# Ten product pairs instead of eight, lookup tables in shared slots, and new planner numbers in a one-core attention block

## The chip, the cores and the metric

The kernel runs as one program on one core of one Trainium2 chip. The time is device microseconds of one execution; lower is better. One core has a tensor engine (PE) with its weight loads (PEld), a vector engine (DVE), a scalar engine (ACT), GpSimd (POOL) and a sync engine (SP) that here issues nearly all DMAs. The engines run their own instruction lists in order and wait for each other through semaphores.

## What is computed

One pre-norm residual block on x (512 tokens x 1024 channels, float32). One projection of the normalised input gives the parts of two attention branches and of their gates; branch A is dense latent attention, branch B keeps the 128 best keys of each query by an indexer's score. The reference, cut to what matters:

```python
h = rmsnorm(x, norm_g[l])
(q_lat, c_kv, k_rope, z_a, q_b, k_b, v_b, z_b,
 q_idx, k_idx, w_idx, gate_a, gate_b) = jnp.split(h @ w_in[l], cuts, axis=-1)
...
y_a = mla_attention(q_nope, q_pe, k_nope, k_pe, v_a, pos) * silu(z_a)
y_b = dsa_attention(q_b, k_b, v_b, q_idx, k_idx, w_idx, rel_bias, pos, topk) * silu(z_b)
merged = sigmoid(gate_a) * (y_a @ w_o_a[l]) + sigmoid(gate_b) * (y_b @ w_o_b[l])
x = x + merged @ w_out[l]
return rmsnorm(x, final_g)
```

## The kernel before

**Precision.** Every float32 operand of a product is split into a rounded high part and the rest (`split_w` L728, `lo_part` L471): ACT writes the high part, DVE or POOL subtracts to get the low part. A product is then three matmuls, high x high, high x low, low x high (`mm3` L500). Activations have channels on the partitions and 512 tokens along the row.

**Single and paired tiles.** A projection tile of 128 output columns taken alone (`proj` L1154) is 8 blocks of channels x 3 = 24 matmuls of 512 columns. Two tiles taken together (`proj2` L1218, `seven` L1304) go through a scheme of seven half-size products instead of eight: 7 x 4 x 3 = 84 matmuls of 256 columns for both. For that, DVE and POOL form sums of weight blocks (`prep` L1243: four additions of 512 columns a pair) and split seven weight blocks where two single tiles have four; the sums of the input are made once (`input_sums` L1185, tiles `s_hs`). ACT and DVE collect the four results in tiles called `s_pair`. The values of branch B (`values2` L1356, VB) are a pair of the same kind with four outputs.

**Stages in the order of time.** Loads of x and of the early weights; indexer scores (`scores` L955) and the choice of keys (`topk` L979: 16 rounds of MAX8 and MATCH_REPLACE for each of three query tiles, on DVE); eight dense heads (`mla_head`, matmuls L1909 to L1911, their row maximum on DVE in L1893); eight sparse heads (`dsa_head`, its row minimum on DVE in L1992); the branch output products (`branch_out`, tiles `s_ys`); the last projection (`output`, tiles `s_wo` and `s_mg`), norm and store. Between the attention matmuls, PE takes projection tiles as filler. The sparse heads start once all three masks are chosen.

**What sets the order.** A planner (`Flow` L154) runs while the program is built. Each piece of work is a Python generator that yields steps; a step has a modelled duration on each engine that may take it. The planner repeatedly emits the step that can start first, with a small tie-break by priority (`PHEAD`, `PSCORE`, `PFILL`, `PTOPK`). So the order of every engine's list follows from the modelled durations, the priorities and the buffers: a shared pool of `NSLOT` = 73 slots of 128x512 floats with caps by use (`WCAP`, `PCAP`, `PHCAP`, `TCAP`, `SPARE`), four raw buffers of 128x1024 for weight loads (`fetcher` L1118), and eight PSUM banks. The modelled PE time is in `stream` (L485), `mm` and `turn` (L507). The order of the projection tiles is the string `QUEUE`: lower case is a single tile, capitals are pairs (SB is the pair of a key and a query tile of branch B).

**Operands of a dense head.** A head's query and key tiles get their rotary rows by small DMAs: `qhi` and `s_op` tiles from `s_th`, `s_op`, `s_qpe` and the shared `kpeh`, `kpel` (`mla_job`). All stand in SP's list, between the weight loads (`raw<-w_...`) and the spills of finished gates to HBM (`bias_scratch<-s_sig`).

Of the kernel before, what the change touches and what calls it, by code (L numbers as in the profile page):

```python
# [36 lines left out]
MARK = -3.4e38  # L37
BIG = 2.0 ** 127
LOW = -(2.0 ** 126)
NSLOT = 73  # L40
NRAW = 4


# [257 lines left out]
def tile_block(ctx: ExitStack, tc: tile.TileContext, a: dict, out: bass.AP, bias_dram: bass.AP):  # L301
# [13 lines left out]
    def fixed(name, shape, dt=F32):  # L315
        return Buf(const.tile(shape, dt, name=name), name)
# [6 lines left out]
        uid[0] += 1  # L323
        return slots.tile([P, S], F32R if cls in rounded else F32, tag=b.name, name=f"{b.name}_{cls}{uid[0]}", bufs=1)

    SB = Pool_([Buf(None, f"s{i}") for i in range(NSLOT)], fresh)
    RAW = Pool_([fixed(f"raw{i}", [P, 1024]) for i in range(NRAW)])
    VV = Pool_([fixed(f"vv{i}", [P, 4, NT, P], F32R) for i in range(2)])

# [93 lines left out]
    BOTH = ("DVE", "POOL")  # L423
# [56 lines left out]
    def pe(time, outs, ins, emit, count=1):  # L480
        step = Step([("PE", time, emit)], bufs(*outs), bufs(*ins))
        step.count = count
        return step

    def stream(n):  # L485
        return max(0.0134 + n / 2400, 0.109)

    def mm(ps, pairs, start, stop, more=False):

# [17 lines left out]
    def turn(parts):  # L507


        def emit():  # L510
            for d, s in parts:
                product_to(d, True)
                nc.tensor.transpose(d.ap, s.ap, ident.tile)  # L513

        return pe(0.0875 * len(parts), [d for d, _ in parts], [s for _, s in parts] + [ident.all], emit, len(parts))

    def dma(dst, src):

# [52 lines left out]
    ident = fixed("ident", [P, P])  # L571
    normg = fixed("normg", [P, NK])
    glat = fixed("glat", [P, 5])
    ropec = fixed("ropec", [P, S])
    ropes = fixed("ropes", [P, S])
    neghalf = fixed("neghalf", [P, 8])
    widx = fixed("widx", [P, NT, 8])

    kpe = [fixed(f"kpe{c}", [68, S], F32R) for c in "hl"]
    mask = [fixed(f"mask{i}", [P, P * (i + 1)]) for i in range(NT)]  # L580
    junk = fixed("junk", [P, S])
    warm = fixed("warm", [P, 8])
    zero = fixed("zero", [P, P // 2])
    ssx = fixed("ssx", [P, 2 * NT])
    rstd = fixed("rstd", [P, NT])
    rb = fixed("rb", [64, NH])
    rbs = fixed("rbs", [P, P], F32R)
    TOK = [slice(t * P, (t + 1) * P) for t in range(NT)]
    LO, HI = slice(0, 256), slice(256, 512)
    SCORED = slice(P, S)  # L590
# [35 lines left out]
    def setup_pool():  # L626
        yield memset("POOL", mask[0].all, 0.0)
        yield memset("POOL", mask[0][0:64, 0:64] if 0 in TURNED else mask[0][0:64, 64:128], MASK)
        yield Until(lambda: 3 in xt)
        yield from pool_dma(ident.all, a["ident"])  # L630
        yield from pool_dma(glat.all, a["g_lat"])
        yield Until(lambda: rbc)
        yield from pool_dma(ropec.all, a["ropec"])
        yield from pool_dma(ropes.all, a["ropes"])
        raw = yield slot("raw")
        rounded_ = yield slot("oh")
        yield from pool_dma(raw.all[0:4, :], a["chunk"][0])
        yield from pool_dma(raw.all[64:68, :], a["chunk"][1])
        yield act(rounded_.all[0:4, :], raw.all[0:4, :])
        yield act(kpe[0].all[64:68, :], raw.all[64:68, :])  # L640
        for q in list(QHI.free):
            yield from pool_dma(q.all.f[96:100, :], rounded_.all.f[0:4, :])
        put(raw, rounded_)
        done.add("rope")
# [78 lines left out]
                tiles.append(xn)  # L723
        done.add("x loads")

    rbc = []

    def split_w(raw, w, dst, key, cls="w", cap=None, release=False, early=False, added=False, high=None):  # L728

# [102 lines left out]
    def normed(k):  # L832
        yield Until(lambda: rbc and k in xg)
        x = getattr(xt[k], "whole", xt[k])
        yield stt(x.all.f, x.all.f, normg[:, k : k + 1], rbc[0].all.f, ALU.mult, ALU.mult)
        hi = yield slot("h")
        lo = yield slot("h")
        yield act(hi.all, x.all.f)
        yield lo_part(lo.all, x.all.f, hi.all)
        if XOUT and k % 4 < NHELD:  # L840
            yield dma(waits(k), x.all.f)
            put(x)
            kept.add(k)
        elif k % 4 < NHELD:
            held[k] = x
        else:
            put(x)
        hT[k] = (hi, lo)

    def square_sum(x, total):  # L850
# [5 lines left out]
        step.pair = True  # L856
        return step

    def rope(dst, src, rows):
        sw = yield slot("tmp", TCAP)  # L860
        yield Until(lambda: "rope" in done)
        yield Step([("DVE", 0.6, lambda: nc.vector.stream_shuffle(sw.all.f[rows].ap, src.ap, SWAP))],
                   [sw], bufs(src))
        yield tt(dst, src, ropec[rows], ALU.mult)
        yield tt(sw.all.f[rows], sw.all.f[rows], ropes[rows], ALU.mult, BOTH)
        yield tt(dst, dst, sw.all.f[rows], ALU.add)
        put(sw)

# [208 lines left out]
    def bias_table():  # L1077
        yield is_done("loads", BIAS_AT)

        yield from pool_dma(rb.all, a["rel_bias"])  # L1080
        yield memset("POOL", rbs.all.f, 0.0)
# [12 lines left out]
        for tp, o, c0, c1 in ((toep, oh[0], 0, 320), (toep2, oh[1], 320, 640)):  # L1094
            ps = yield bank("pv")
            yield pe(0.148, [ps.all], [rbs.all, o.all], lambda: (product_to(ps[:, :320], True), nc.tensor.matmul(
                ps.tile[:, :320], rbs.tile, o.tile[:, :320], start=True, stop=True)))
# [4 lines left out]
        put(*oh, toep, toep2)  # L1102
        done.add("bias")


# [12 lines left out]
    def fetcher():  # L1118
        yield is_done("loads")
        for job in jobs:  # L1120
            raw = yield Get(RAW)
            dst = raw[:, : sum(job.widths)]
            if len(job.src.shape) == 3:
                dst = dst.re("p (b c) -> p b c", b=job.src.shape[1])
            yield dma(dst, job.src)
            job.raw = raw
# [348 lines left out]
    sig = {}  # L1475
# [1023 lines left out]

# [80 lines left out]
```

## Time and profile before

| | |
|---|---|
| median of 3 runs | 428.67 us (427.9 to 429.76) |
| profiled execution | 429.5 us, its span 427.7 us |
| mean granted TensorE clock | 0.991 |
| ACT busy | 293.5 us (69%) |
| POOL busy | 101.6 us (24%) |
| DMA | 65.91 MB, mean 154 GB/s |

The span runs from the first instruction to the last one of one profiled execution; 1.8 us of that execution lie around it. Busy time of PE is a union of matmuls that overlap in the pipeline, so it shows whether PE had work, not how fast it went; the number of matmuls in a stretch that has no gap shows that.

### The profile page before, as it was taken

What the parts mean: (1) busy time and instruction counts of PE and PEld (TensorE: products, weight loads), DVE (VectorE), ACT (ScalarE), POOL (GpSimd) and SP (SyncE); (2) the same over time, 40 slices, a digit from 0 to 9 for tenths busy, and PEclk for the clock granted to TensorE, in tenths of its full rate; (3) what the DMA queues carried; (4) which work ended last, traced back from release to release, by engine and by line L of the source; (5) the groups of instructions that cost most, each with busy time, mean ns of one, the idle gap of its engine ahead of it and who ended that gap; (6) DMA issues with size and microseconds to landing.
All of it is one profiled execution on the core that took longest, in us unless ns stands there. A gap on an engine that the chain in (4) does not pass through costs nothing.

```text
span 427.7 us, 7455 instructions
## 1 busy us (share of the span) xinstructions
PE 415.5 (97%) x2451; PEld 369.4 (86%) x2451; DVE 375.5 (88%) x801; ACT 293.5 (69%) x669; POOL 101.6 (24%) x126
## 2 busy tenths in 40 slices
PE   8999999899999999999999999999999999999993
PEld 6989888698888888888999998999988888888882
DVE  4869779589999999998969959999989876999994
ACT  5876986368685847648857698898689643348534
POOL 1032856122854442811112002111000000000212
PEclk9999999989999999999999999999999999999998
DMA  8982645605645361350243644522583884458105
GB/s 260 396 311 69 163 116 154 179 2 129 193 123 159 99 203 49 94 166 25 100 149 111 183 140 103 157 64 85 164 267 125 263 280 171 172 163 329 50 1 197
DMA packets 30279, 65.91 MB, mean 154 GB/s; under 512 B 4648, under 2 KB 5688, under 8 KB 30240
## 3 DMA queue, kind: packets, MB, share of 16 engines
q1 hardware_dynamic: 29120, 63.82, 47.2%
q0 software_dynamic: 832, 1.22, 1.0%
q8 instruction: 19, 0.31, 0.3%
q10 hardware_dynamic: 288, 0.39, 0.3%
q14 instruction: 20, 0.16, 0.1%
HBM read 50.49 MB, written 4.21 MB: 128 GB/s over the span
## 4 chain that ended last, share of the span: by engine, by line
PE 63%; DVE 17%; DMA 9%; ACT 5%; issue 3%; SPq 2%; POOL 0%; POOLq 0%; ACTq 0%; DVEq 0%
PE ps L494 54%; PE ps L513 5%; DVE s_w L416 2%; DVE s_wo L416 2%; DMA raw<-w_o 2%; DVE s_mg L416 2%; ACT s_w L381 2%; SPq L523 2%; DMA s_op<-kpel 1%; DMA raw<-w_ql 1%; DMA s_x<-xT 1%; DMA s_xn<-x 1%; DVE s_pair L416 1%; DVE s_rg L416 1%; PE ps L1910 1%
## 5 line engine op out<-in xcount | busy, mean ns | idle before, releaser
L494 PE MATMUL ps<-s_h,s_w 128*128 128x512 f32 (+1 forms) x684 | 149.5, 357 | 1.1 <-ACT s_pair L381 0.6
L494 PEld LDWEIGHTS ps<-s_h,s_w 128*128 128x128 f32 x684 | 110.3, 189 | 15.6 <-ACT s_pair L381 1.5
L381 ACT CAST s_w<-raw 128x512 fp32r<-128x512 f32 (+3 forms) x132 | 76.0, 595 | 22.0 <-DMA raw<-w_o 12.7
L416 DVE TENSOR_TENSOR s_w<-raw,s_w 128x512 fp32r<-128x512 f32 (+2 forms) x95 | 62.1, 674 | 3.9 <-ACT s_w L381 3.5
L418 POOL TENSOR_TENSOR s_w<-raw,s_w 128x512 fp32r<-128x512 f32 (+2 forms) x37 | 44.5, 1207 | 61.7 <-ACT s_w L381 30.7
L494 PE MATMUL ps<-s_hs,s_w 128*128 128x256 f32 x336 | 46.7, 285 | 0.0
L494 PE MATMUL ps<-s_ys,s_w 128*128 128x512 f32 x192 | 43.9, 389 | 0.0
L494 PEld LDWEIGHTS ps<-s_hs,s_w 128*128 128x128 f32 x336 | 42.8, 191 | 0.4 <-DVE s_w L416 0.2
L494 PEld LDWEIGHTS ps<-s_ys,s_w 128*128 128x128 f32 x192 | 36.0, 188 | 7.4
L494 PE MATMUL ps<-s_w,s_xg 128*128 128x328 f32 (+1 forms) x192 | 33.1, 325 | 0.3 <-ACT s_rbc L381 0.2
L494 PE MATMUL ps<-s_wo,s_mg 128*128 128x512 f32 (+1 forms) x156 | 33.0, 373 | 0.0
L494 PEld LDWEIGHTS ps<-s_w,s_xg 128*128 128x128 f32 x192 | 31.3, 188 | 1.2 <-ACT s_rbc L381 0.5
L494 PEld LDWEIGHTS ps<-s_wo,s_mg 128*128 128x128 f32 x156 | 27.6, 188 | 5.2
L390 ACT ACTIVATE s_p<-ps,sm 128x128 f32<-128x128 f32 (+3 forms) x32 | 16.9, 528 | 17.7 <-DVE sm L1893 17.5
L390 ACT ACTIVATE s_p<-s_p,sm 128x512 f32<-128x512 f32 (+3 forms) x52 | 28.7, 571 | 0.1
L986 DVE MAX8 sm<-mask 128x8 f32<-128x256 f32 (+2 forms) x48 | 25.6, 550 | 0.6 <-POOL mask L568 0.2
L987 DVE MATCH_REPLACE8 mask<-sm,mask 128x256 f32<-128x256 f32 (+2 forms) x48 | 26.0, 543 | 0.1
L513 PE MATMUL ps<-ident,s_p 128*128 128x128 f32 x160 | 23.1, 274 | 0.0
L494 PE MATMUL ps<-s_lat,s_w 128*128 128x512 f32 x78 | 20.7, 397 | 0.0
L513 PEld LDWEIGHTS ps<-ident,s_p 128*128 128x128 f32 x160 | 18.5, 140 | 2.1
L1992 DVE CUSTOM_DVE_ANT_0 s_p<-ps,mask 128x128 f32<-128x128 f32 (+3 forms) x32 | 15.1, 488 | 5.7 <-PE ps L494 5.3
L418 POOL TENSOR_TENSOR s_pair<-s_pair 128x256 f32<-128x256 f32 x1 | 0.7, 743 | 81.2 <-issue 81.2
(213 smaller groups left out, 800.2 us busy)
## 6 DMA issues: line engine op xcount, KB each, us to landing
raw<-w_out SPq DMA_DIRECT2D x18, 512.0 KB, 4.6
s_op<-s_op SPq DMA_DIRECT2D x36, 128.0 KB, 2.7
raw<-w_ga SPq DMA_DIRECT2D x8, 512.0 KB, 4.3
raw<-w_gb SPq DMA_DIRECT2D x8, 512.0 KB, 4.3
raw<-w_o SPq DMA_DIRECT2D x16, 256.0 KB, 3.1
s_x<-xT SPq DMA_DIRECT2D x8, 256.0 KB, 4.0
s_xn<-x SPq DMA_DIRECT2D x8, 256.0 KB, 5.7
raw<-w_za SPq DMA_DIRECT2D x4, 512.0 KB, 4.8
```

Source lines behind the costliest of these rows:

```text
L381: nc.scalar.copy(dst.ap, src.ap)
L390: nc.scalar.activation(dst.ap, src.ap, func, **kw)
L416: opts.append(("DVE", 0.07 + 0.00104 * x.n + few(x), lambda: nc.vector.tensor_tensor(dst.ap, x.ap, y.ap, op=op)))
L418: opts.append(("POOL", 0.15 + 0.0021 * x.n, lambda: nc.gpsimd.tensor_tensor(dst.ap, x.ap, y.ap, op=op)))
L494: nc.tensor.matmul(ps.ap, l.ap, r.ap, start=start and i == 0, stop=stop and i == len(pairs) - 1, skip_group_check=more)
L513: nc.tensor.transpose(d.ap, s.ap, ident.tile)
L523: return Step([("SP", n / 360000.0, lambda: nc.sync.dma_start(d, s))], bufs(dst), bufs(src))
L986: yield Step([("DVE", t, lambda: nc.vector.max(m8.tile, work.ap))], [m8], [mask[i]])
L987: yield Step([("DVE", t - 0.009, lambda: nc.vector.match_replace(work.ap, m8.tile, work.ap, MARK))], [mask[i]], [m8])
L1910: nc.tensor.matmul(o, q0[0:96], k1[0:96], start=False, stop=False)
L1992: step = Step([("DVE", 0.1 + 0.00104 * n, lambda: nc.vector.tensor_tensor_reduce(p.ap, ps.tile[:, :n], mask[i].tile, op0=ALU.add, op1=ALU. ...
```

## The change

It has four parts.

1. **Pairs.** In `QUEUE` the single tiles ga6, ga7, zb0 and zb3 become halves of pairs: GA6 with GA7, ZB0 with ZB1, ZB2 with ZB3 (before, ZB1 went with ZB2). There are ten pairs, VB and the four SB among them, where there were eight. GA6 and GA7's pair stands behind SB1.
2. **Buffers.** The two rotary tables and the table for the bias no longer have tiles of their own but take slots for as long as they are used; the tile `junk` is BF16; the count of slots is 78. Weight loads of up to 512 columns (`w_va`, `w_o`) take a slot called `ro` (three at most) where they took one of the four raw buffers.
3. **Modelled PE times.** A transpose of 128 columns is 0.109 us (before 0.0875), and the other matmuls get 1.4 ns more, those of 256 columns 0.1 ns less.
4. **Other planner numbers**: priorities, caps, and from where on POOL and ACT are preferred.

```diff
-NSLOT = 73
+NSLOT = 78
...
     def stream(n):
-        return max(0.0134 + n / 2400, 0.109)
+        return max(0.0148 + n / 2400, 0.109) - 0.0015 * (n == 256)
...
-        return pe(0.0875 * len(parts), [d for d, _ in parts], [s for _, s in parts] + [ident.all], emit, len(parts))
+        return pe(0.109 * len(parts), [d for d, _ in parts], [s for _, s in parts] + [ident.all], emit, len(parts))
...
-    ropec = fixed("ropec", [P, S])
-    ropes = fixed("ropes", [P, S])
...
-    junk = fixed("junk", [P, S])
+    junk = fixed("junk", [P, S], BF16)
...
-        yield from pool_dma(ropec.all, a["ropec"])
-        yield from pool_dma(ropes.all, a["ropes"])
+        for name in ("ropec", "ropes"):
+            t = yield slot("rope")
+            yield from pool_dma(t.all.f, a[name])
+            turns.append(t)
...
-            raw = yield Get(RAW)
+            raw = (yield slot("ro", ROCAP)) if sum(job.widths) <= S and ROCAP else (yield Get(RAW))
...
-QUEUE = 'ga0 ga1 pe ma0 ga2 za0 va1 va0 ma1 ga3 za1 ma2 ga4 ga5 ma3 za2 za3 sb0 zb0 ga6 ga7 VB SB1 GB0 GB1 SB2 ZB1 ZB2 GB2 GB3 SB3 GB4 GB5 zb3 gb6 ou ou gb7 ou'
+QUEUE = 'ga0 ga1 pe ma0 ga2 za0 va1 va0 ma1 ga3 za1 ma2 ga4 ga5 ma3 za2 za3 sb0 VB SB1 GA6 GA7 GB0 GB1 SB2 ZB0 ZB1 GB2 GB3 SB3 GB4 GB5 ZB2 ZB3 gb6 ou ou gb7 ou'
...
-PTOPK = 13.0
-PSCORE = 10.0
-PFILL = 12.0
-PHEAD = 4.0
+PTOPK = 17.0
+PSCORE = 3.0
+PFILL = 14.0
+PHEAD = 8.0
...
-YSB = 5
+YSB = 6
```

The numbers not shown: `PHCAP` and `TCAP` 5 to 7, `WCAP` 12 to 11, `PCAP` 11 to 10, `SPARE['w']` 3 to 2, `PSUMS` 8 to 10, `SUMS_AT` one dense head earlier, `NORM_ABIAS` -0.4 to -0.2, `LATE` 0.4 to 0.2. In the changed file the lines of the dense heads are L1922 to L1924 (maximum L1906) and the sparse minimum is L2005.

**SP, the operands of the first two dense heads, before.** Behind the row of `s_qpe_979`, a weight load for the next heads, a load of a gate's weights and a gate's spill stand among the small DMAs; `s_op_984` and `s_op_986` are the key tiles of the first head.

```order
L523 DMA s_op_992<-s_qpe_979 32x512
L523 DMA raw_68<-w_uqkv 128x640
L523 DMA s_op_984<-kpeh 36x512
L523 DMA raw_69<-w_ga 128x1024
L523 DMA bias_scratch<-s_sig_1053 128x512
L523 DMA s_op_986<-kpel 32x512
L523 DMA s_op_1024<-kpeh 36x512
L523 DMA s_op_1026<-kpel 32x512
```

**The same place of the changed kernel**; `s_op_987` and `s_op_989` are now the first head's key tiles.

```order
L523 DMA qhi_73<-s_qpe_963 32x512
L523 DMA s_op_987<-kpeh 36x512
L523 DMA s_op_970<-s_qpe_964 32x512
L523 DMA qhi_72<-s_qpe_963 32x512
L523 DMA s_op_1001<-s_qpe_964 32x512
L523 DMA s_op_989<-kpel 32x512
L523 DMA s_op_1009<-kpeh 36x512
L523 DMA s_op_1011<-kpel 32x512
L523 DMA bias_scratch<-s_sig_1062 128x512
L523 DMA raw_67<-w_ga 128x1024
```

The small DMAs of both heads now stand together; the spill and the gate's weights have moved behind them, and `w_uqkv` ahead of the block.

**DVE ahead of the first tile of the first sparse head (the ISA row), before.** `s_hs` and `s_tmp` belong to the sums of the input, `s_wsum` to VB's weights.

```order
L416 TENSOR_TENSOR s_hs_2309<-s_x_149,s_hs_2308 128x512
L416 TENSOR_TENSOR s_wsum_2320<-raw_66,raw_69 128x512
L416 TENSOR_TENSOR s_hs_2324<-s_x_166,s_hs_2323 128x512
L416 TENSOR_TENSOR s_tmp_2331<-s_h_579,s_h_580 128x512
L416 TENSOR_TENSOR s_tmp_2336<-s_h_629,s_h_630 128x512
L416 TENSOR_TENSOR s_tmp_2331<-s_tmp_2331 128x256
L416 TENSOR_TENSOR s_wsum_2321<-raw_66,raw_69 128x512
L1992 ISA s_p_2296,sm_86<-ps_99,mask_109 128x128
```

**The same place of the changed kernel**; `s_op_2691` and `s_op_2692` are SB1's results, `raw_67` and `raw_68` hold the weights of ga6 and ga7.

```order
L416 TENSOR_TENSOR s_op_2691<-s_pair_2453,s_op_2690 128x512
L428 SCALAR_TENSOR_TENSOR s_op_2692<-s_pair_2455,qhi_74 128x512
L416 TENSOR_TENSOR s_w_2685<-s_wsum_2597,s_w_2684 128x512
L416 TENSOR_TENSOR s_w_2701<-raw_66,s_w_2700 128x512
L416 TENSOR_TENSOR s_wsum_2742<-raw_67 128x512
L416 TENSOR_TENSOR raw_67<-raw_67,raw_68 128x512
L416 TENSOR_TENSOR s_w_2721<-raw_69,s_w_2720 128x512
L416 TENSOR_TENSOR s_w_2740<-raw_68,s_w_2739 128x512
L416 TENSOR_TENSOR raw_68<-s_wsum_2742,raw_68 128x512
L2005 ISA s_p_2664,sm_90<-ps_98,mask_107 128x128
```

Before, VB's weights were only begun here; now the work of VB and SB1 is behind DVE and GA6 and GA7's has begun. Counted in the lists from the first dense tile to the first sparse tile, PE has 821 rows where it had 572 (376 matmuls of 256 columns where it had 82, 283 of 512 where it had 327), and DVE 263 where it had 209 (74 two-input operations of 128x512, TENSOR_TENSOR, where it had 24).

**PE at the first sparse tile, before and then changed**: `s_h`, `s_hs` are the input, `s_op`, `qhi` a sparse head.

```order
L494 MATMUL ps_95<-s_h_630,s_w_2149 128x512
L494 MATMUL ps_95<-s_h_629,s_w_2151 128x512
L494 MATMUL ps_99<-s_op_2184,qhi_72 128x128
L494 MATMUL ps_99<-s_op_2213,qhi_72 128x128
L494 MATMUL ps_93<-s_h_522,s_w_2190 128x512
```

```order
L494 MATMUL ps_94<-s_hs_2104,s_w_2644 128x256
L494 MATMUL ps_94<-s_hs_2300,s_w_2644 128x256
L494 MATMUL ps_98<-s_op_2164,qhi_72 128x128
L494 MATMUL ps_98<-s_op_2199,qhi_72 128x128
L494 MATMUL ps_95<-s_h_592,s_w_2655 128x256
```

Around it stood matmuls of single tiles; now those of pairs do.

More of the change, by code (lines that the diff above doesn't have):

```diff
@@ L324, in fresh @@
         return slots.tile([P, S], F32R if cls in rounded else F32, tag=b.name, name=f"{b.name}_{cls}{uid[0]}", bufs=1)
-    SB = Pool_([Buf(None, f"s{i}") for i in range(NSLOT)], fresh)
+    SB = Pool_([Buf(None, f"s{i}") for i in range(NSLOT + 8 - 2 * NRAW)], fresh)
     RAW = Pool_([fixed(f"raw{i}", [P, 1024]) for i in range(NRAW)])
@@ L586, in tile_block @@
     rb = fixed("rb", [64, NH])
-    rbs = fixed("rbs", [P, P], F32R)
     TOK = [slice(t * P, (t + 1) * P) for t in range(NT)]
@@ L724, in x_squares, with rbc_done @@
         done.add("x loads")
-    rbc = []
+    rbc, rbc_users = [], [NK + 2]
+    def rbc_done():
+        rbc_users[0] -= 1
+        if not rbc_users[0]:
+            put(rbc[0])
     def split_w(raw, w, dst, key, cls="w", cap=None, release=False, early=False, added=False, high=None):
@@ L835, in normed @@
         yield stt(x.all.f, x.all.f, normg[:, k : k + 1], rbc[0].all.f, ALU.mult, ALU.mult)
+        rbc_done()
         hi = yield slot("h")
@@ L857, in square_sum @@
         return step
+    turns, turn_users = [], [3]
     def rope(dst, src, rows):
@@ L863, in rope @@
                    [sw], bufs(src))
-        yield tt(dst, src, ropec[rows], ALU.mult)
-        yield tt(sw.all.f[rows], sw.all.f[rows], ropes[rows], ALU.mult, BOTH)
+        c, sn = turns
+        yield tt(dst, src, c.all.f[rows], ALU.mult)
+        yield tt(sw.all.f[rows], sw.all.f[rows], sn.all.f[rows], ALU.mult, BOTH)
+        turn_users[0] -= 1
+        if not turn_users[0]:
+            put(c, sn)
         yield tt(dst, dst, sw.all.f[rows], ALU.add)
@@ L910, in take_qi @@
             yield tt(tmp.all.f[:, SCORED], banks[m][:, SCORED], rbc[0].all.f[:, SCORED], ALU.mult)
+            rbc_done()
             put(banks[m])
@@ L1078, in bias_table @@
         yield is_done("loads", BIAS_AT)
+        rbs = yield slot("oh")
         yield from pool_dma(rb.all, a["rel_bias"])
-        yield memset("POOL", rbs.all.f, 0.0)
+        yield memset("POOL", rbs[:, :P].f, 0.0)
         yield act(rbs[0:64, 0:NH], rb.all)
@@ L1096, in bias_table @@
             yield pe(0.148, [ps.all], [rbs.all, o.all], lambda: (product_to(ps[:, :320], True), nc.tensor.matmul(
-                ps.tile[:, :320], rbs.tile, o.tile[:, :320], start=True, stop=True)))
+                ps.tile[:, :320], rbs.tile[:, :P], o.tile[:, :320], start=True, stop=True)))
             yield act(tp.all.f[:NH, : c1 - c0], ps[:NH, : c1 - c0] if BADD else backward(ps[:NH, : c1 - c0]))
@@ L1101, in bias_table @@
             yield from pool_dma_out(bass.AP(bias_dram.tensor, c0 if BADD else NREL - c1, [[NREL, NH], [1, c1 - c0]]), tp.all.f[:NH, : c1 - c0])
-        put(*oh, toep, toep2)
+        put(rbs, *oh, toep, toep2)
         done.add("bias")
@@ L2445 @@
 NORM = ('DVE', 'POOL', 'ACT')
-NORM_ABIAS = -0.4
+NORM_ABIAS = -0.2
 NORM_B = ('DVE', 'ACT')
@@ L2451 @@
 QPOOL = 1
-PHCAP = 5
-WCAP = 12
-TCAP = 5
-PTOPK = 13.0
-PSCORE = 10.0
-PFILL = 12.0
-PHEAD = 4.0
+PHCAP = 7
+WCAP = 11
+TCAP = 7
+PTOPK = 17.0
+PSCORE = 3.0
+PFILL = 14.0
+PHEAD = 8.0
 OUT_AT = (2, 3, 5, 10, 10, 10, 14)
 ORDER = [0,1,2,3]
-QUEUE = 'ga0 ga1 pe ma0 ga2 za0 va1 va0 ma1 ga3 za1 ma2 ga4 ga5 ma3 za2 za3 sb0 zb0 ga6 ga7 VB SB1 GB0 GB1 SB2 ZB1 ZB2 GB2 GB3 SB3 GB4 GB5 zb3 gb6 ou ou gb7 ou'
-LATE = 0.4
+QUEUE = 'ga0 ga1 pe ma0 ga2 za0 va1 va0 ma1 ga3 za1 ma2 ga4 ga5 ma3 za2 za3 sb0 VB SB1 GA6 GA7 GB0 GB1 SB2 ZB0 ZB1 GB2 GB3 SB3 GB4 GB5 ZB2 ZB3 gb6 ou ou gb7 ou'
+LATE = 0.2
 EARLY = (1, 7, 2)
@@ L2489 @@
 PREST = 8.0
-SPARE = {'w': 3, 'wo': 6, 'sig': 3}
+SPARE = {'w': 2, 'wo': 6, 'sig': 3}
 XOUT = 0
-PSUMS = 8.0
-PCAP = 11
+PSUMS = 10.0
+PCAP = 10
 BIAS_AT = ('a', 1)
 NHELD = 3
-SUMS_AT = ('a', 6)
+ROCAP = 3
+SUMS_AT = ('a', 5)
 AWAY = (0, 1, 2, 3, 4, 5, 6, 7)
```

## The prediction

> **What bounds the kernel now.** I read the page's sums first.
>
> ```profile
> span 427.7 us, 7455 instructions
> PE 415.5 (97%) x2451; PEld 369.4 (86%) x2451; DVE 375.5 (88%) x801; ACT 293.5 (69%) x669; POOL 101.6 (24%) x126
> ```
>
> PE is busy 415.5 of 427.7 us, so at most 12.2 us are not PE work. The windows say where DVE, second at 375.5 us, comes near it (columns: stretch, its length, busy time with count of PE, PEld, DVE, ACT, POOL, granted clock, DMA share, GB/s).
>
> ```profile
> 0.00:85.20 85.20, 81.54 (x437) 71.83 (x437) 64.10 (x129) 60.07 (x134) 32.17 (x47) 1.00 0.64 207
> 85.20:193.10 107.90, 107.83 (x573) 92.67 (x572) 104.34 (x255) 72.20 (x172) 47.56 (x59) 0.98 0.42 121
> ...
> 134.50:158.30 23.80, 23.80 (x129) 20.39 (x128) 23.51 (x57) 16.52 (x40) 10.50 (x12) 1.00 0.55 162
> ...
> 193.10:249.00 55.90, 55.89 (x435) 54.06 (x434) 50.05 (x96) 42.16 (x95) 7.24 (x6) 1.00 0.38 116
> 249.00:270.30 21.30, 20.66 (x161) 19.63 (x160) 17.75 (x47) 18.62 (x49) 2.60 (x2) 1.00 0.46 124
> ...
> 338.00:381.50 43.50, 43.50 (x195) 36.12 (x195) 37.34 (x65) 16.24 (x28) 0.74 (x1) 1.00 0.60 206
> ...
> 381.50:420.40 38.90, 38.88 (x194) 32.88 (x192) 38.71 (x75) 22.54 (x50) 5.07 (x6) 1.00 0.35 126
> 420.40:427.70 7.30, 0.00 (x0) 0.00 (x0) 1.97 (x6) 2.89 (x6) 1.06 (x2) 0.71 0.71 266
> ```
>
> The second row is the dense heads with the choice of keys; 193.10 is the first sparse tile, 420.40 the last matmul. PE has no gap from 85.2 to 193.1, but DVE is busy 104.34 of those 107.90 us: 3.56 us idle. In 134.50:158.30 it is busy 23.51 of 23.80 and PE still never waits. So DVE this full costs nothing so far; there is also little left. From 193.1 on DVE has 10% free and more, until the last projection. The tail of 7.3 us is norm and store; the change doesn't touch it.
>
> PE's own loss worth a look stands just ahead of 85.2, in PE's timeline (start, length, engine, line; in brackets the wait ahead and who ended it) and in windows of PE alone (length, busy, granted clock).
>
> ```profile
> 82.94 0.22 PE L1909 MATMUL ps<-s_op,qhi 100*128 100x128 f32 x1
> 85.00 0.33 PE L1910 MATMUL ps<-s_op,qhi 96*128 96x128 f32 x1 [1.84 <-DMA s_op<-kpel]
> ```
>
> ```profile
> 85.00:86.00 1.00, 1.00 (x7) 0.80 0.00 0
> 86.00:87.00 1.00, 1.00 (x6) 0.50 0.00 0
> ...
> 88.00:89.00 1.00, 1.00 (x7) 0.50 0.06 16
> 89.00:90.00 1.00, 1.00 (x10) 0.99 0.00 0
> ```
>
> The first head's second matmul waits 1.84 us for a small DMA. Behind it the granted clock is 0.80, then 0.50 for three windows, then 0.99: 0.20 + 3 x 0.50 + 0.01 = 1.7 us of PE work lost. **The wait costs 1.84 + 1.7 = 3.5 us.** The 0.64 us of the next row, a wait for ACT, lie in 249.00:270.30, where the granted clock stays 1.00: a wait that short costs itself alone.
>
> ```profile
> 257.11 0.63 PE L494 MATMUL ps<-s_h,s_w 128*128 128x256 f32 x3 [0.64 <-ACT s_pair L381]
> ```
>
> The skill's rule would price this otherwise. The Trainium skill, "TensorE: Matmul & The Clock Gate", section "What's actually happening", has the clock halve after about 3.4 us idle and come back after about 3.4 us busy. By it 1.84 us idle would halve nothing, the wait would be worth 1.84 and the forecast below 1.7 us higher, 427.6. The trace differs on the idle time and agrees on the way back (0.50 for about 3.5 us); I go by the trace.
>
> **The change, term by term. 1: PE's work.** The lists of before and after differ by 168 more matmuls of 256 columns and 96 fewer of 512 (one more pair in place of two single tiles is 84 for 48, and there are two more pairs), and one 512-column matmul that only writes zeros is gone. Rates from stretches without a gap:
>
> ```profile
> 211.04 3.04 PE L494 MATMUL ps<-s_w,s_h 128*128 128x256 f32 x24
> 213.92 1.36 PE L494 MATMUL ps<-s_w,s_hs 128*128 128x256 f32 x10
> ```
>
> ```profile
> L494 PE MATMUL ps<-s_ys,s_w 128*128 128x512 f32 x192 | 43.9, 389 | 0.0
> ```
>
> 24 of 256 columns take 213.92 - 211.04 = 2.88 us, 0.120 each; 192 of 512 take 43.9, 0.229 each. 168 x 0.120 = 20.2; 97 x 0.229 = 22.2. **Term: -2.0 us.** It holds wherever PE has no gap.
>
> **2: the wait.** SP's timeline, and the chain and the page on the transfers (start and time to landing; size and median time to landing):
>
> ```profile
> 76.25 0.58 SPq L523 DMA_DIRECT2D raw<-w_uqkv  x1
> 76.93 0.85 SPq L523 DMA_DIRECT2D s_op<-kpeh  x1
> 77.89 0.40 SPq L523 DMA_DIRECT2D raw<-w_ga  x1
> 78.35 0.42 SPq L523 DMA_DIRECT2D bias_scratch<-s_sig  x1
> 78.82 0.58 SPq L523 DMA_DIRECT2D s_op<-kpel  x1
> ```
>
> ```profile
> 78.82 6.14 DMA s_op<-kpel
> ```
>
> ```profile
> s_op<-s_op SPq DMA_DIRECT2D x36, 128.0 KB, 2.7
> raw<-w_ga SPq DMA_DIRECT2D x8, 512.0 KB, 4.3
> ```
>
> `s_op<-kpel` left at 78.82 behind 512 KB of `w_ga` and a spill, and took 6.14 us where a small operand's median is 2.7. In the new order both stand behind the operands. Without them it leaves 78.82 - 77.89 = 0.93 earlier, at 77.9, and lands at about 80.6. PE has 9 rows fewer ahead of the first dense tile (433 for 442); at 0.229 that is 2.1 us, so it wants the tile at 83.2 - 2.1 = 81.1. The margin is 0.5 us. The term lies between 0 (still late, or another operand is) and -3.5. **I take -3.5**, the row of a small operand's usual time being the nearest; half a microsecond late would give back only that. `w_ga` and the spill, now later, feed filler tiles and free a slot: no wait of PE in this stretch rests on them.
>
> **3: DVE in the dense heads.** Two pairs more are 14 two-input operations of 512 columns more in all (four weight sums and three more low parts each). But the order also pulls VB, SB1 and part of GA6 with GA7 ahead of the first sparse tile. By the counts with the order, PE gets there 294 matmuls of 256 more, 44 of 512 and one of 384 fewer: 294 x 0.120 - 44 x 0.229 - 0.2 = +25.0 us. DVE gets 50 operations of 512 and three of 256 more. Their spacing, from DVE's timeline:
>
> ```profile
> 377.95 0.69 DVE L416 TENSOR_TENSOR s_pair<-s_pair,s_sig 128x512 f32<-128x512 f32 x1
> 378.56 0.69 DVE L416 TENSOR_TENSOR s_mg<-s_pair,s_mg 128x512 fp32r<-128x512 f32 x1
> 379.16 0.42 DVE L416 TENSOR_TENSOR s_mgsum<-s_pair,s_pair 128x256 f32<-128x256 f32 x1
> ...
> 380.43 0.42 DVE L416 TENSOR_TENSOR s_mgsum<-s_pair,s_pair 128x256 f32<-128x256 f32 x1
> 380.77 0.42 DVE L416 TENSOR_TENSOR s_pair<-s_pair,s_mgsum 128x256 f32<-128x256 f32 x1
> ```
>
> Starts are 379.16 - 378.56 = 0.60 us apart behind one of 512 columns and 0.34 behind one of 256: 50 x 0.60 + 3 x 0.34 = 31 us. So the stretch wants:
>
> - PE: 107.9 - 1.7 (clock, term 2) + 25.0 = 131.2 us
> - DVE: 104.3 + 31 = 135.3 us of work, 4.1 more than PE has
>
> In before DVE had less work than PE there by 3.6 us, now it has more by 4.1. The lower bound of the cost is 0: in 134.50:158.30 DVE is at 99% and PE never waits, and PE has 25 us more of filler in the stretch, with which it can run ahead of a late sum. Below zero nothing speaks for it, as the matmuls are counted in term 1. With DVE never idle the stretch takes 4.1 longer, with the 3.56 idle of before kept 7.7. **I take +2.7**, two thirds of the way from 0, which a row shows for a stretch with a smaller surplus, to 4.1, which is a sum of work that has to be done. What is late in the stretch isn't made up later: PE has next to no gap there to shrink.
>
> **4: the rest.** The tables' slots, the BF16 `junk` and the `ro` slots add no instruction on PE or DVE; ACT has 31% free and covers its own. POOL has 11 two-input operations of 512 fewer. Behind the first sparse tile PE has 25 us less filler than before, and DVE, at 50.05 of 55.90 in the first stretch there, has the room that it lost ahead. If the filler ran out at a head, PE would wait as it does in the row of 257.11, 0.6 us a time. **Term: 0.**
>
> **Sum.** -2.0 - 3.5 + 2.7 = **-2.8 us**. The profiled execution took 429.5 us (span 427.7, 1.8 around it): 426.7. It lies 0.8 above the median of 428.67; against that, **425.9 us**.
>
> **Rivals.**
>
> *DVE becomes the bound (slower).* With 135.3 us of work, the 3.56 us of idle kept, and the 50 new operations held up beside POOL as those with a weight block and its rounded part are against those that only add two weight blocks:
>
> ```profile
> L416 DVE TENSOR_TENSOR s_w<-raw,s_w 128x512 fp32r<-128x512 f32 x79 | 54.2, 703 | 3.1 <-ACT s_w L381 2.6
> L416 DVE TENSOR_TENSOR s_wsum<-raw 128x512 f32<-128x512 f32 x15 | 10.2, 682 | 0.0
> L418 POOL TENSOR_TENSOR s_w<-raw,s_w 128x512 fp32r<-128x512 f32 x29 | 37.6, 1298 | 59.9 <-ACT s_w L381 30.0 <-ACT s_ph L381 13.4 <-ACT ps L381 3.9
> ```
>
> Mean 703 ns against 682: 50 x 0.02 = 1.0. 135.3 + 3.6 + 1.0 = 139.9 against PE's 131.2: +8.7. Sum -2.0 - 3.5 + 8.7 = +3.2: **431.9**. It decides once DVE's lag passes the gain of 5.5 us, and gives over 0.5% from 7.6. For it: the sums. Against: at 99% DVE cost PE nothing, and PE holds whole tiles of filler that need no fresh DVE row. The Trainium skill, "SBUF — State Buffer", section "SBUF: two separate sides", adds that GpSimd and a two-input vector operation exclude each other for a whole instruction; at 1298 ns for one of POOL's a held-up row would show about 1.3 us, and the 703 mean says that few are.
>
> *The wait stays (same).* The margin of term 2 is 0.5 us, and the other operands of the head must land too. If one is late by as much as before, -2.0 + 2.7 = +0.7: **429.4**. This is also the case in which the change doesn't do what its order promises.
>
> *DVE costs nothing (faster).* Term 3 at 0: -5.5, **423.2**.
>
> **How the numbers follow.** Forecast 425.9, chance 0.45, own range 424.2 to 427.3 (term 3 from +1 to +4.1). DVE bound 0.20, wait stays 0.23, DVE free 0.12. A measurement of this kernel tells 0.5% from no change, so faster is below 426.5, slower above 430.8. Faster: 0.33 of the forecast's 0.45, and the 0.12: 0.45. Same: 0.12 + 0.20 + 0.02 = 0.34. Slower: 0.18 of DVE's and 0.03 of the wait's: 0.21. The range reaches down past most of DVE free (422.5) and up past the DVE bound's 431.9 (432.5), which leaves about 2 in 10 out.
>
> **What would show it.** Term 1: 84 matmuls of 256 in about 10.1 us where a new pair runs without a gap. Term 2: no wait above 0.6 us at L1922 and L1923 and a granted clock of 1.00 behind; a wait for another operand's DMA says the rival. Term 3: from the first dense to the first sparse tile 131 us if DVE is free, 134 as I say, about 140 if it binds, with PE waits that DVE's `s_w` or `s_wsum` ends. It is wrong if a gap opens after the first sparse tile, where I price none, or if PE waits at the last heads.

## The result, and the profile after

| | before | changed |
|---|---|---|
| median | 428.28 us (4 runs, 427.28 to 429.76) | 423.72 us (4 runs, 423.12 to 424.0) |
| ratio | | 0.9889, interval 0.9857 to 0.9921 |
| profiled execution | 429.5 us, span 427.7 | 423.12 us, span 421.3 |
| granted TensorE clock | 0.991 | 0.995 |

The changed kernel is 1.1% faster: 4.6 us by the medians, 6.4 us by the two profiled executions. It lies inside the predicted range and below the forecast's own range, next to the rival in which DVE costs nothing.

The page's sums of the changed kernel:

```profile
span 421.3 us, 7603 instructions
PE 412.3 (98%) x2522; PEld 369.7 (88%) x2522; DVE 385.6 (92%) x822; ACT 298.4 (71%) x692; POOL 91.3 (22%) x116
```

The windows by stage (length, busy time with count of PE, PEld, DVE, ACT, POOL, granted clock, DMA share, GB/s). The second row runs from the first dense tile to the first sparse tile, the third to the last sparse tile, the fourth to the last matmul.

```profile
0.00:82.00 82.00, 80.21 (x426) 70.13 (x427) 67.62 (x134) 60.97 (x136) 32.27 (x48) 1.00 0.62 206
82.00:215.20 133.20, 132.95 (x823) 118.11 (x821) 132.00 (x305) 88.03 (x208) 44.17 (x53) 1.00 0.40 117
215.20:328.10 112.90, 112.90 (x869) 109.23 (x868) 101.22 (x227) 100.33 (x248) 6.47 (x5) 1.00 0.54 158
328.10:414.40 86.30, 86.26 (x410) 72.24 (x409) 82.77 (x153) 46.11 (x96) 7.24 (x8) 1.00 0.46 158
414.40:421.30 6.90, 0.00 (x0) 0.00 (x0) 1.95 (x6) 2.95 (x6) 1.10 (x2) 0.67 0.75 284
```

DVE is busy 132.00 of 133.20 us in the second row and PE still has no gap to speak of. At the first dense head PE's timeline now reads:

```profile
81.98 0.23 PE L1922 MATMUL ps<-s_op,qhi 100*128 100x128 f32 x1
82.04 0.27 PE L1923 MATMUL ps<-s_op,qhi 96*128 96x128 f32 x1
82.15 0.28 PE L1924 MATMUL ps<-s_op,s_op 96*128 96x128 f32 x1
```

No wait stands in brackets. PE's waits, before and then changed (who waited, for whom, us in total, times, longest):

```profile
PE ps L1910 <- DMA s_op<-kpel: 1.8, 1, 1.8
...
PE ps L494 <- ACT s_pair L381: 0.6, 1, 0.6
```

```profile
PE ps L618 <- DVE neghalf L568: 1.0, 1, 1.0
PE ps L513 <- POOL rstd L468: 0.2, 1, 0.2
PE ps L494 <- ACT s_pair L381: 0.2, 1, 0.2
PE ps L494 <- ACT s_w L381: 0.2, 1, 0.2
```

The 1.0 us for `neghalf` is PE's first wait of all; the kernel before has it too.

What became of the small DMA that ended the 1.8 us, the first head's `kpel` operand (size, and us from issue to landing), before and then changed:

```profile
s_op<-kpel SPq DMA_DIRECT2D x1, 64.0 KB, 6.1
```

```profile
s_op<-kpel SPq DMA_DIRECT2D x1, 64.0 KB, 1.9
```

It left at 78.78 us, no earlier than before (78.82), but landed at 80.67, 1.3 us ahead of the first dense tile at 81.98.

To see where the 6.4 us of the two profiles went, each stretch is split in two: what its matmuls take at their rates without a gap (0.120 us for 256 columns, 0.229 for 512, 0.1745 for 384, 0.149 for 328, 0.109 for 128), and the rest, called stall here (waits, a lowered clock, small delays).

| stretch, from matmul to matmul | before: length (stall) | changed: length (stall) |
|---|---|---|
| first matmul to first dense tile | 82.0 (3.4) | 81.0 (3.9) |
| to the first sparse tile | 110.1 (4.8) | 133.2 (2.9) |
| to the last sparse tile | 134.0 (3.2) | 113.0 (0.6) |
| to the last matmul | 93.1 (-0.6) | 86.0 (-0.6) |
| tail behind it | 7.4 | 7.0 |

The matmuls alone fall from 408.4 to 406.4 us (the lengths without the tail, 419.2 and 413.2, less the stalls 10.8 and 6.8): -2.0. The stall falls by 4.0: +0.5, -1.9 and -2.6 in the first three rows. The tail gives the last 0.4. Two things in it were not in the forecast: the stall between the sparse heads went, 2.6 us, and the stall of the dense stretch fell by 1.9 where terms 2 and 3 together gave 0.8.

### The profile page after: what moved, and what is told of

The parts are those of the page before. It is cut to its first block, busy times and chain, and to the rows that moved or that the text cites. A ratio compares the mean times of both kernels' runs of the same rounds, so it can differ in the third digit from the quotient of the medians.

```text
span 421.3 us, 7603 instructions
## 1 busy us (share of the span) xinstructions
PE 412.3 (98%) x2522; PEld 369.7 (88%) x2522; DVE 385.6 (92%) x822; ACT 298.4 (71%) x692; POOL 91.3 (22%) x116
## 4 chain that ended last, share of the span: by engine, by line
PE 77%; DVE 12%; issue 8%; ACT 1%; POOL 1%; POOLq 0%; DVEq 0%; ACTq 0%
PE ps L494 68%; PE ps L513 5%; DVE s_w L416 1%; PE ps L1922 1%; DVE s_rg L416 1%; DVE mask L999 1%; DVE s_xr L428 1%; DVE s_wo L416 1%; DVE sm L998 1%; PE ps L1923 1%; PE ps L1924 1%; PE ps L973 1%; DVE mask L428 1%; DVE s_xr L416 1%; DVE raw L416 1%
## 5 line engine op out<-in xcount | busy, mean ns | idle before, releaser
L494 PE MATMUL ps<-s_h,s_w 128*128 128x512 f32 (+1 forms) x660 | 131.7, 342 | 0.2 <-ACT s_pair L381 0.2
L494 PEld LDWEIGHTS ps<-s_h,s_w 128*128 128x128 f32 x660 | 102.4, 189 | 11.9 <-ACT s_pair L381 0.6
L381 ACT CAST s_w<-raw 128x512 fp32r<-128x512 f32 (+2 forms) x118 | 69.0, 595 | 8.7 <-DVE raw L416 7.6
L494 PE MATMUL ps<-s_hs,s_w 128*128 128x256 f32 x432 | 60.7, 285 | 0.0
L494 PEld LDWEIGHTS ps<-s_hs,s_w 128*128 128x128 f32 x432 | 55.6, 191 | 0.4
L418 POOL TENSOR_TENSOR s_w<-raw,s_w 128x512 fp32r<-128x512 f32 (+2 forms) x25 | 28.6, 1146 | 22.8 <-ACT s_w L381 14.7
L390 ACT ACTIVATE s_p<-s_p,sm 128x256 f32<-128x256 f32 (+3 forms) x59 | 31.5, 553 | 1.7 <-DVE sm L1869 1.6
L418 POOL TENSOR_TENSOR s_wsum<-raw 128x512 f32<-128x512 f32 x4 | 5.2, 1301 | 100.3 <-PE ps L513 63.3
L381 ACT COPY s_pair<-ps 128x256 f32<-128x256 f32 (+1 forms) x40 | 15.7, 392 | 10.4 <-PE ps L494 10.2
L416 DVE TENSOR_TENSOR s_ph<-ps,s_ph 128x512 fp32r<-128x512 f32 (+1 forms) x32 | 19.2, 620 | 1.9 <-ACT s_ph L381 1.8
```

Source lines behind the costliest of these rows:

```text
L381: nc.scalar.copy(dst.ap, src.ap)
L390: nc.scalar.activation(dst.ap, src.ap, func, **kw)
L416: opts.append(("DVE", 0.07 + 0.00104 * x.n + few(x), lambda: nc.vector.tensor_tensor(dst.ap, x.ap, y.ap, op=op)))
L418: opts.append(("POOL", 0.15 + 0.0021 * x.n, lambda: nc.gpsimd.tensor_tensor(dst.ap, x.ap, y.ap, op=op)))
L494: nc.tensor.matmul(ps.ap, l.ap, r.ap, start=start and i == 0, stop=stop and i == len(pairs) - 1, skip_group_check=more)
```

## The experiments

Where an edit says "order alone", one engine's list is permuted at one place and everything else stands as it was. The others plan anew, so the whole order may change. All comparisons are to 23 or 16 runs of the kernel before made beside them (428.22, 428.2 and 427.8 us), and the changed kernel's ratio of 0.9889 is the yardstick; differences in us from the changed kernel are differences of medians.

### The kernel before, once more

> The kernel of before once more, for a second profile. If the wait of the first dense head is a property of the order, L1910 waits again 1.5 to 2.2 us for the small DMA from kpel and the granted clock falls to 0.5 for about 3 us behind it. If it was a mishap of one execution, wait or clock drop are absent here and the term of 3.5 us in the forecast stood on one profile alone.

429.33 us, and the wait is there:

```profile
PE ps L1910 <- DMA s_op<-kpel: 1.5, 1, 1.5
```

```profile
84.00:86.00 2.00, 1.42 (x10) 0.88 0.01 5
86.00:88.00 2.00, 2.00 (x11) 0.50 0.04 8
88.00:90.00 2.00, 2.00 (x15) 0.77 0.02 4
```

(windows of PE alone: length, busy, granted clock). 1.5 us of waiting, then a clock of 0.50: 2 x 0.12 + 2 x 0.50 + 2 x 0.23 = 1.7 us lost, as in the first profile. But the runs of this kernel made beside all the experiments, 62 in all, fall in two groups by their mean granted clock: 17 at 0.993 or less, median 429.97 us, and 45 at 0.994 or more, median 427.68. Both profiles are of the first group. The wait stands in both profiles; the lowered clock, by these groups, in about 3 of 10. No profile shows an execution of the second group, so what the wait was there isn't seen.

### The operands first

> The kernel of before with one edit: on SP the load of w_ga and the spill of a gate are issued behind the key operands of the first two dense heads; every other list is unchanged. Theory (the forecast's term 2): no wait above 0.5 us at L1910, granted clock 1.00 from 85 to 90 us, and 3.5 us less, so about 425.0 for 428.5. Rival 1, the idle time counts but not the clock: 1.8 us less, 426.7. Rival 2, another operand or the delayed w_ga is late next: less than 1 us less.

```diff
 s_op<-kpeh
-raw<-w_ga
-bias_scratch<-s_sig
 s_op<-kpel
 s_op<-kpeh
 s_op<-kpel
+raw<-w_ga
+bias_scratch<-s_sig
```

Order alone. 426.46 us over 12 runs, ratio 0.9959 (0.9940 to 0.9979): 1.8 us less. The profiled execution took 426.12, 3.2 less than the one above. PE's timeline and the clock behind it:

```profile
82.96 0.23 PE L1909 MATMUL ps<-s_op,qhi 100*128 100x128 f32 x1
83.02 0.28 PE L1910 MATMUL ps<-s_op,qhi 96*128 96x128 f32 x1
```

```profile
85.00:90.00 5.00, 5.00 (x35) 1.00 0.02 5
```

The wait is gone and nothing is late in its place: `w_ga` and the spill cost nothing behind. The dense stretch fell from 110.1 to 106.7 us and the other stretches stayed within 0.2. `kpel` now left at 77.79 us and landed 2.4 us later. So the mechanism of term 2 holds; against the two profiles that had lost clock the gain is 3.2 and 3.4, by the median it is 1.8, which is the expectation of rival 1. None of the 12 runs has a clock under 0.994. Against the two groups of the kernel before, the median of 426.46 is 3.5 us less than the first and 1.2 less than the second, so the 1.8 is a mixture of executions and not one price.

### The operands late again in the changed kernel

> The changed kernel with one edit: on SP the gate's spill and one load of w_ga are issued ahead of the last three key operands of the first two dense heads, as in the kernel of before. Theory: a wait of about 2 us is back at L1923, the clock falls behind it, and the time rises by 3.5 us to about 427.2. Rival: the operands still land in time, or a short wait of under 0.7 us leaves the clock at 1.00, and the time rises by less than 0.7 us.

```diff
 s_op<-s_qpe
+bias_scratch<-s_sig
+raw<-w_ga
 s_op<-kpel
 s_op<-kpeh
 s_op<-kpel
-bias_scratch<-s_sig
-raw<-w_ga
```

Order alone. 428.87 us over 12 runs, ratio 1.0005 (0.9982 to 1.0028), 5 us more than the changed kernel.

```profile
82.44 0.23 PE L1922 MATMUL ps<-s_op,qhi 100*128 100x128 f32 x1
85.80 0.33 PE L1923 MATMUL ps<-s_op,qhi 96*128 96x128 f32 x1 [3.13 <-DMA s_op<-kpel]
```

```profile
86.00:90.00 4.00, 4.00 (x28) 1.00 0.00 0
```

The wait is longer than the one of before, as `w_ga`'s load goes out 2.9 us later here and `kpel` 2.6. In this execution 3.13 us of idle lowered no clock. The 12 runs go from a clock of 0.996 and 427.12 us to 0.987 and 429.46, with 8 at 0.993 or less. That this order decides over some 5 us in the changed kernel is shown. Whether an idle time lowers the clock is not a matter of its length alone.

### VectorE spared

> The changed kernel in which 34 subtractions of 512 columns (the low parts of weight blocks and of input sums that VectorE makes between the first dense and the first sparse tile) are left out: a copy of the high part, with one input, stands in their place, so those products use the high part twice. Order and waits for the high part are the same; VectorE is spared 34 x (0.60 - 0.33) = 9 us in the stretch. Theory (VectorE at 99% there costs TensorE about 1.5 us in small waits): 1 to 2 us less. Rival 1, VectorE is free in the stretch: no change within 0.3 us. Rival 2, VectorE binds there: 4 us less or more.

```diff
-... lambda: nc.vector.tensor_tensor(dst.ap, x.ap, y.ap, op=op)))
+... lambda: nc.vector.tensor_copy(dst.ap, y.ap) if _low(dst, x, op) else nc.vector.tensor_tensor(dst.ap, x.ap, y.ap, op=op)))
```

423.94 us, ratio 0.9890 (0.9863 to 0.9917): no change. The same window as above:

```profile
82.00:215.20 133.20, 132.74 (x824) 118.39 (x823) 123.97 (x305) 88.35 (x208) 44.15 (x53) 1.00 0.40 118
```

DVE is busy 8.0 us less and the stretch takes 133.2 us as before. Rival 1 holds: at 99% DVE costs nothing that the median shows, and most of the 2.9 us of stall in the stretch isn't its doing (2.8 here). The profile leaves room for some 0.4 us: PE's wait of 0.2 us for `s_pair` at 208.87 is gone, and a wait of 0.4 us for a small DMA, `s_op<-kpeh` at 131.77, is new.

### VectorE loaded

> The changed kernel with 13 reductions of 32 x 512 added on VectorE, one every twentieth step between the first dense and the first sparse tile, whose results nothing uses: some 0.5 us each, 6.5 us in all. The run with 34 shorter operations showed that VectorE at 99% costs nothing there. Theory A (it is full, and the next microsecond counts): the stretch has 1.2 us of VectorE idle left, so 4 to 5.3 us more, about 428.5. Theory B (what is late on VectorE at the end of the stretch is work for tiles behind it, and TensorE has filler): less than 1.5 us more.

```diff
+    if eng == "DVE" and n in MORE:
+        nc, to, x = EXTRA
+        nc.vector.tensor_reduce(to.tile[32:64, 0:1], x.all.f[32:64, :].ap, op=ALU.max, axis=AX.X)
```

434.18 us, ratio 1.0133 (1.0094 to 1.0173): 10.5 us more. Each reduction took 675 ns, and in the trace the next operation starts 0.71 us behind its start, so the 13 are 9.2 us of work.

> The changed kernel with 5 added reductions on VectorE (every sixtieth step between the first dense and the first sparse tile, 0.60 us each from start to start, 3.0 us in all) where the run with 13 (7.8 us) lost 10.5 us. Theory (VectorE and TensorE are level in this stretch, and any more work on VectorE is lost one for one or worse): 3 to 4 us more, about 427.3. Rival (a first microsecond or two is free): under 1.5 us more, about 424.5.

427.31 us, ratio 0.9987 (0.9969 to 1.0006): 3.6 us more by the medians, 4.2 by the ratios. The expectation counted 0.60 us for each reduction; with the 0.71 of the trace the five are 3.5 us of work. The windows from first dense to first sparse tile, of the run with 5 and of the run with 13:

```profile
82.00:218.20 136.20, 134.20 (x823) 117.77 (x821) 134.90 (x309) 87.84 (x208) 45.33 (x53) 1.00 0.39 115
```

```profile
82.00:224.60 142.60, 136.17 (x823) 117.52 (x821) 140.90 (x317) 87.88 (x208) 44.90 (x53) 1.00 0.38 110
```

Four rows of this window tell it together: DVE's work of 124.0, 132.0, 134.9 and 140.9 us goes with stretches of 133.2, 133.2, 136.2 and 142.6. From 132 on the stretch is DVE's work plus 1.2 to 1.7; in the one run below, it stays at PE's 133.2. **The changed kernel stands on the corner.** Of PE's waits in the run with 13, the largest is

```profile
PE ps L1922 <- ACT s_p L390: 2.7, 5, 0.8
```

the next dense tile's wait for a bank that ACT's exponential still reads, and that exponential takes DVE's row maximum.

### The planner's parts, one at a time

Five runs plan anew with one part of the change taken alone or undone. The new buffers were neither taken alone nor undone.

> The kernel of before with only the modelled PE times of the change (transposes 0.109 us, the others 1.4 ns more or 0.1 ns less); its SP list still has the load of w_ga and the spill ahead of the first head's kpel operand, and its pairs are the eight of before. Theory (the waits for s_pair among the sparse heads, 2.6 us of the gain, go because the planner now knows when PE is done): between the first and the last sparse tile the stall over the matmuls' own rate falls from 3.3 to about 0.7 us, the wait at L1910 stays, and the time falls by 2 to 2.6 us to about 426. Rival (those waits go through the pairs or the other numbers): the stall there stays above 2.5 us and the time within 0.7 us of 428.2.

```diff
-        return max(0.0134 + n / 2400, 0.109)
+        return max(0.0148 + n / 2400, 0.109) - 0.0015 * (n == 256)
...
-        return pe(0.0875 * len(parts), [d for d, _ in parts], [s for _, s in parts] + [ident.all], emit, len(parts))
+        return pe(0.109 * len(parts), [d for d, _ in parts], [s for _, s in parts] + [ident.all], emit, len(parts))
```

433.98 us, ratio 1.0121 (1.0088 to 1.0154): 5.8 us slower, where 2 less was expected. The stall between the sparse heads is 4.5 us, not 0.7, and longer waits stand ahead of the heads (1.3 us for `rstd`, 0.4 before) and in the last projection (1.5 for `s_wo`, none before).

> The kernel of before with only the changed queue of tiles: ten pairs; the SP list at the first dense head, the modelled times and the other numbers are those of before. Theory (term 1 of the forecast): 2.0 us less through fewer PE columns, about 426.2, with the wait at L1910 as before and DVE above 98% busy from the first dense to the first sparse tile without a cost. Rival (the pairs need the other edits too): new waits for ACT or DVE eat the gain, 428 or more.

```diff
-... za3 sb0 zb0 ga6 ga7 VB SB1 GB0 GB1 SB2 ZB1 ZB2 GB2 GB3 SB3 GB4 GB5 zb3 gb6 ...
+... za3 sb0 VB SB1 GA6 GA7 GB0 GB1 SB2 ZB0 ZB1 GB2 GB3 SB3 GB4 GB5 ZB2 ZB3 gb6 ...
```

445.14 us, ratio 1.0365 (1.0324 to 1.0405): 17 us slower. PE waits for a sum of the input in the middle of a pair:

```profile
187.66 1.22 PE L494 MATMUL ps<-s_w,s_hs 128*128 128x256 f32 x4
192.26 0.80 PE L494 MATMUL ps<-s_w,s_hs 128*128 128x256 f32 x2 [3.38 <-ACT s_hs L381]
```

The dense stretch has 12.2 us of stall, the sparse one 7.1. Part of the former is clock: behind an earlier wait of 1.96 us for `s_w` (it ends at 184.85) the granted clock is 0.50 from about 186.5 to 196 us, through the 3.38 us shown.

> The changed kernel with only the queue of tiles of before: eight pairs; the SP list at the first dense head is that of the changed kernel. Theory: 2.0 us more than the changed kernel through more PE columns, about 425.7, no wait at L1923 and a granted clock of 1.00 there, DVE in the dense stretch back at about 97%. Rival (the pairs are worth more, through relief elsewhere, or less): more than 3 us or less than 1 us more.

The same edit the other way round. 430.51 us, ratio 1.0049 (1.0027 to 1.0070): 6.8 us more than the changed kernel, of which 2.0 are PE's columns. The sparse stretch has 1.0 us of stall, but from the last sparse tile to the first product of the branch outputs 3.9 us are new, where PE has no filler left and waits for single steps of the last head.

> The changed kernel planned with the modelled PE times of before; pairs, buffers and other numbers are the changed ones; the load of w_ga stays behind the first heads' operands. Theory (what took the waits out of the sparse heads is the planner's PE times together with the other numbers): the stall between the first and the last sparse tile goes from 0.6 to over 2 us. Rival (the other numbers alone did it): it stays under 1.2 us there, and a slower total comes from other places.

This edit undoes more than the change made: it also sets the modelled time of 128-column matmuls that share their weights to 0.0134 us and n / 2400, which is 0.0148 and n / 2400 in both kernels. 439.15 us, ratio 1.0249 (1.0217 to 1.0282): 15.4 us more. The sparse stretch has 5.8 us of stall, and PE waits 3.7 us for `s_hs` in the dense one.

```profile
PE ps L494 <- ACT s_hs L381: 3.7, 1, 3.7
PE ps L494 <- ACT ps L381: 3.5, 1, 3.5
```

The 3.5 us for `ps` stand at the last sparse tile and are most of the sparse stall. Behind both waits the granted clock fell to 0.50, for about 3 us behind the first and about 10 us around and behind the second; the four runs' mean clocks are 0.978 to 0.985. So this run's time is in good part two long waits and the clock behind them.

> The changed kernel planned with the other planner numbers of before (priorities, caps, preferences); pairs, buffers and modelled PE times are the changed ones. On SP a load of w_ga then stands ahead of the first head's kpel operand again. Theory: the wait at L1923 of 1 us or more is back, and the stall between the first and the last sparse tile goes from 0.6 to over 2 us; 427 or more. Rival (the numbers matter little beside pairs and modelled times): within 1 us of 423.7.

432.88 us, ratio 1.0116 (1.0089 to 1.0142): 9.2 us more. The sparse stall is 3.0 us. The largest loss lies in the dense stretch, which has 9.1 us of stall: one wait of 4.2 us, with a clock of 0.50 for about 3 us behind it.

```profile
186.86 3.36 PE L494 MATMUL ps<-s_w,s_hs 128*128 128x256 f32 x16 [4.23 <-DVE s_w L416]
```

The wait at L1923 didn't come back, though a load of `w_ga` stands ahead of `kpel`: SP issues it at 75.97 and `kpel` at 76.56, 4.4 us ahead of the first dense tile at 80.95, where the kernel of before had 4.1. Here the spill stands behind the operands; how much of the late landing was `w_ga`'s and how much the spill's was not separated.

### The waits of the sparse heads

> The kernel of before with the SP edit of the earlier run, and two places of ScalarE's list changed: a copy of a product's result to s_pair stands ahead of two softmax operations (at 256 us), another ahead of one cast (at 300 us), where PE waited 0.8 and 0.6 us for those copies. Theory (the waits of the sparse heads come from where such copies stand on ScalarE): both waits shrink to under 0.4 us, and 0.8 us less than the run with the SP edit alone, about 425.7. Rival (the softmax or the cast is then late for PE in their place): no difference beyond 0.3 us.

```diff
+COPY s_pair<-ps
 ACTIVATE s_p<-s_p,sm 128x512
 ACTIVATE s_p<-s_p,sm 128x384
-COPY s_pair<-ps
...
+COPY s_pair<-ps
 CAST s_w<-raw
-COPY s_pair<-ps
```

Order alone, on top of the SP edit. 427.34 us, ratio 0.9974 (0.9958 to 0.9991), 0.9 more than the SP edit alone (the intervals overlap). ScalarE's and PE's timelines at the two places:

```profile
253.14 0.37 ACT L381 COPY s_pair<-ps 128x256 f32<-128x256 f32 x1 [1.06 <-PE ps L494]
```

```profile
253.57 1.10 PE L494 MATMUL ps<-s_h,s_w 128*128 128x256 f32 x7 [0.46 <-ACT s_pair L381]
...
298.19 0.97 PE L494 MATMUL ps<-s_h,s_w 128*128 128x256 f32 x6 [0.98 <-ACT s_w L381]
```

The first copy now waits 1.06 us for PE's product, and PE still waits 0.46 for the copy where it waited 0.63 in the run with the SP edit alone. At the second place the expectation had misread the wait: in the kernel of before PE waits there for the cast and not for the copy,

```profile
300.66 1.10 PE L494 MATMUL ps<-s_h,s_w 128*128 128x256 f32 x7 [0.44 <-ACT s_w L381]
```

and with the cast pushed back by the copy it waits 0.98. So at the first place the copy's position on ScalarE explains at most 0.2 us of the wait, and the second place wasn't put to the test. No run here settles the cause. The stall of the sparse stretch is 0.6 and 1.0 us in the two plans that have both the new PE times and the new numbers, and 3.2, 4.5, 7.1, 5.8 and 3.0 in the five that lack one of them, the kernel of before among them. But the two share the new buffers as well, and in the five it is not one wait that comes back: 0.6 for `s_pair` and 0.4 for `s_w` in the kernel of before, 3.5 for `ps` where the PE times are undone, 1.4 for `s_w` and 1.2 for `s_ph` where the queue is taken alone. This is a pattern over seven plans, not a cause.

## Why the prediction was right, and where it was wrong

**Term 1, PE's work, -2.0 us.** The traces have the matmuls that the lists promised, 168 more of 256 columns and 97 fewer of 512, and at the forecast's rates that is -2.0 again. This is its own arithmetic on confirmed counts; no run takes the term alone. (Of the ten pairs three are SB pairs, not four: `sb0` is two single tiles in both kernels. The count of ten is right.)

**Term 2, the wait, -3.5 us.** The cause was right: `kpel` behind `w_ga` and the spill, its removal without a late wait in its place, and the return of the wait when the order is put back. The steps were not all as forecast. It was to leave 0.93 us earlier and to land at 80.6 for a tile at 81.1; in the changed kernel it left at the same time as before, landed at 80.67 because it took 1.9 us where it had taken 6.1, and PE came to the tile at 81.98. The size was off. The step that failed is "the wait costs 1.84 + 1.7 = 3.5 us": the idle time stands in both profiles, the 1.7 of clock is lost in about 3 executions of 10, and the median gains 1.8. One profile had been read as the rule. The Trainium skill, "TensorE: Matmul & The Clock Gate", section "What's actually happening", says that the window of the clock gate is free-running, so that the moment at which the clock changes depends on where in the window the matmuls begin. Two groups of runs of one program would fit that; no run here shows the window. On the idle time the traces differ from its rule of about 3.4 us: 1.5, 1.8 and 2.0 us were enough in three executions here. Idle times of 3.5, 3.7 and 4.2 us lowered the clock too, and one of 3.1 did not.

**Term 3, DVE, +2.7 us.** Wrong: it cost nothing to speak of, as the run that spares it shows. The forecast's own sign would have misled here: it gave 131 us for the stretch if DVE is free and 134 as forecast, and the stretch took 133.2 with DVE free. Two steps failed. The sum of 135.3 us counted what the list gains and nothing of what it loses; the added operations did cost 30.7 us in the trace (29.7 for 48 of 512 columns, 1.0 for three of 256), but the stretch also lost two scalar-tensor operations of 512 columns and one of 384, and the choice of keys cost 1.8 us less. In all DVE's work there is 27.0 us more, 132.3 in all when each operation counts to the start of the next, and so less than the 133.2 that the stretch takes even with DVE spared. And the choice of two thirds of a surplus treated as a slope what is a corner: nothing from 124 to 132 us of DVE work, and about one for one above. The rival "DVE becomes the bound" was therefore not far off: 3.5 us more of DVE work would have cost 3.6.

**Term 4, the rest, 0.** Wrong by 2.6 us, the stall between the sparse heads. It was set at nothing because the waits there (0.6 us for `s_pair` in the quoted row) were read as small change that any order has. With the 0.4 for `s_w` they make 1.0 of the 3.2 us of stall; the rest is many small delays, which the forecast didn't look for. That they went is measured. The replanned runs suggest that it takes the new PE times and the other numbers together, but they don't show it, and through which step is open. This is the largest single piece of the gain.

**The sum.** -2.0, -3.5 and +2.7 gave -2.8. Measured in the medians' terms: -2.0 of work, -1.8 for the wait, -2.6 between the sparse heads, and in the profiles +0.5 at the start, -0.4 in the tail, and about +1.5 of small stalls in the longer dense stretch (2.9 us against the 1.4 that remain there in the kernel of before with the operands first), -4.8 beside the -4.6 of the medians. The 1.5 us are in the main not DVE's and were not traced further. The time of the rival "DVE costs nothing", 423.2, was met to 0.5 us, partly by errors that cancel: its wait was priced 1.7 too high and the sparse heads' 2.6 were not in it.

**The rival "the wait stays"** fell. The margin was not the 0.5 us of the forecast but 1.3, as PE came to the tile 0.9 us later than reckoned.

## What to carry to other kernels

Price a wait from several executions: the idle time came back, the clock lost behind it did not always. Ask what stands ahead of a small DMA, and not only when it leaves: it left at the same time in both kernels. Where two engines are level in a stretch, sum what a change takes from the second engine's list as well as what it adds, and expect a corner, not a slope. Before moving an instruction out of the way, read at its own place which one is waited for. Parts of a planner's change don't add up: the five replanned runs that had one part alone or lacked one were all slower than the kernel before (0.5 to 3.7%), though the whole was 1.1% faster.

## What the runs showed of the hardware

The granted TensorE clock fell to 0.50 after idle times of 1.5 us (the kernel before, once more), 1.8 (the kernel before), 2.0 (the queue alone), 3.5 and 3.7 (PE times undone) and 4.2 (numbers undone). It stayed at 1.00 after 0.8 (the queue alone), 0.9 (PE times alone) and 3.1 (operands late again). The same program, 62 times, splits by its mean granted clock in two groups 2.3 us apart.

A DMA of 64 KB took 6.1 us to land behind a load of 512 KB and a spill of 256 KB, and 2.4 us in the same kernel with those two behind it.
